# Expert weights in an MoE stage: successive rows to a partition, and transposes that read strided columns

## The chip, the cores and the metric

The kernel runs on one NeuronCore of one Trainium2 chip. The metric is the device time of one execution in microseconds (us); the time of a kernel is the median of several executions. All numbers are float32 at the kernel's boundary. Engines carry the names of the profile: PE is TensorE's matrix multiplication, PEld its weight loading, DVE VectorE, ACT ScalarE, POOL GpSimd, SP SyncE, which here only issues DMA transfers.

## The reference

The reference is a small network: a first block (two kinds of attention, a mixture of experts, a gate) and two hybrid layers. The change touches the mixture of experts alone:

```python
def expert_block(args):
    xb, e = args
    hdn = jax.nn.silu(xb @ w1[e]) * (xb @ w3[e])
    return hdn @ w2[e]
```

There are 1024 tokens of width 1024 and 32 experts; a router sends each token to two of them. `w1[e]` and `w3[e]` are 1024 x 512, `w2[e]` is 512 x 1024. `xb` holds up to 128 tokens of one expert. All weights of all experts are read once: 32 x 6 MB = 192 MB.

## The kernel before, in words

**Order of the work.** The kernel is written in the Tile framework. An automatic scheduler, which simulates a timeline, sets the order of instructions on each engine; the program gives the work in the order of `moe`'s loop, and the scheduler moves it where dependences and buffers allow.

**Rows of an expert.** For expert e, `gather` (L925) fetches its 128 token rows into `xg` with an indirect DMA on POOL's queue, two buffers in turn. `expert` then transposes them: eight 128x128 transposes on PE (L887), four to a PSUM bank, where block k takes the columns k*128 to k*128+127 of `xg`. The result is split into two float32r numbers that add up to it: ACT copies the high half to `exh` (L869), DVE subtracts for the low half `exl` (L871).

**Weights.** Each matrix comes as two tiles of 1 MB (128 partitions x 2048 numbers), named a and b here: for `w1` and `w3` the upper and lower 512 rows, for `w2` the left and right 512 columns. `fetch` has `load_raw` issue one DMA per tile on SP's queue (L122): row k*128+p of the tile goes to partition p, so each partition gets four runs of 2 KB. The raw tiles lie in seven buffers that take turns. `split` (PIECES = 4) cuts a tile into four pieces of 128x512; ACT copies the high half (L113), DVE subtracts the low one (L114). The halves go to two buffers `whi`/`wlo` in turn, or to the single buffer `mhi`/`mlo`; every third tile takes the latter. For an expert that gives: w1b to `m`, w3b to `w`, the next expert's w1a to `w` and w3a to `m`, w2a and w2b to `w`.

**Matmuls.** `mm` (L877 to L879) does one product of 128 rows in three matmuls of 512 columns: high x high, high rows x low weights, low rows x high weights. `w1` and `w3` take 8 x 3 each. ACT forms silu into `esg` (L904, two halves), DVE multiplies into `ehd` (L905, two halves); PE transposes `ehd` (four times, L910), which is split into `ehh` and `ehl` by the same lines L869 and L871. For `w2` there are two column halves c, each with a PSUM bank of its own: four k of three matmuls, then ACT copies the bank into `ey` (L919). POOL scatters the finished `ey` to DRAM with an indirect DMA (L920).

**The loop.** `moe` runs in its body for expert e: the transposes of e+1; w1b and w3b of e with `esg`, `ehd` and its transposes; w1a and w3a of e+1; in e = 4 to 11 a tile of other work (PLE, L643 ff); then w2a and w2b of e. `overflow` holds a loop for experts with over 128 rows; with these data it runs zero times. PSUM has five banks for matmuls and three for transposes.

Of the kernel before, what the change touches and what calls it, by code (L numbers as in the profile page):

```python
# [7 lines left out]
F32 = mybir.dt.float32  # L8
F32R = mybir.dt.float32r
I32 = mybir.dt.int32  # L10
AF = mybir.ActivationFunctionType
# [25 lines left out]
PLACE = (4, 7, 8)  # L37


MOE_RAW, MOE_HL, MOE_DMA, PIECES, PLE = 3, 1, 1, 4, 4  # L40

LATE = 7

# [1 line left out]
class Kernel:  # L45
# [70 lines left out]
    def load_raw(self, raw, src, kt, n, dma=2):  # L116

        raw = raw[:, :kt * n].rearrange("p (k n) -> p k n", n=n)
        s = src.rearrange("(k p) n -> p k n", p=128)
        st = kt // dma  # L120
        for j in range(dma):
            self.wdma = self.nc.sync.dma_start(raw[:, j * st:(j + 1) * st], s[:, j * st:(j + 1) * st])  # L122
        return raw

    def w_raw(self):
# [736 lines left out]
    def expert(self, wp, xg, w1, w3, w2, sidx, native, after=None):  # L862


        nc = self.nc
        dt = F32 if native else F32R

        def put(hi, lo, p):
            nc.scalar.activation(hi, p, AF.Copy)  # L869
            if not native:  # L870
                nc.vector.tensor_sub(lo, p, hi.bitcast(F32))  # L871

        def mm(ps, a, k, w, first, last):
            if native:
                nc.tensor.matmul(ps, a[0][:, k], w, start=first, stop=last)
                return
            nc.tensor.matmul(ps, a[0][:, k], w[0], start=first, stop=False)  # L877
            nc.tensor.matmul(ps, a[0][:, k], w[1], start=False, stop=False)
            nc.tensor.matmul(ps, a[1][:, k], w[0], start=False, stop=last)  # L879

        xh = wp.tile([128, 8, 128], dt, name="exh", bufs=1 if native else 2)
        xl = xh if native else wp.tile([128, 8, 128], F32R, name="exl", bufs=2)
        for hf in range(2):
            p = self.t_ps()
            for j in range(4):
                k = hf * 4 + j
                nc.tensor.transpose(p[:, j * 128:j * 128 + 128], xg[:, k * 128:k * 128 + 128], self.ident)  # L887
            put(xh[:, hf * 4:hf * 4 + 4].rearrange("p a t -> p (a t)"),
                xl[:, hf * 4:hf * 4 + 4].rearrange("p a t -> p (a t)"), p)
        yield  # L890
        qs = [self.mm_ps() for _ in range(2)]
        for c in range(2):
            for w, q in zip((w1, w3), qs):
                ww = w(c)
                for k in range(4):
                    mm(q, (xh, xl), c * 4 + k, ww[:, k] if native else (ww[0][:, k], ww[1][:, k]), c + k == 0, c + k == 4)
            if c == 0:
                yield
        hd = wp.tile([128, 512], F32, name="ehd", bufs=1)
        sg = wp.tile([128, 512], F32, name="esg", bufs=1)  # L900
        for c in range(2):
            cs = slice(c * 256, c * 256 + 256)
            with self.tc.issue_after(after.ins) if after else nullcontext():
                nc.scalar.activation(sg[:, cs], qs[0][:, cs], AF.Silu)  # L904
            nc.vector.tensor_mul(hd[:, cs], qs[1][:, cs], sg[:, cs])  # L905
        hh = wp.tile([128, 4, 128], dt, name="ehh", bufs=1)
        hl = hh if native else wp.tile([128, 4, 128], F32R, name="ehl", bufs=1)
        p = self.t_ps()
        for j in range(4):
            nc.tensor.transpose(p[:, j * 128:j * 128 + 128], hd[:, j * 128:j * 128 + 128], self.ident)  # L910
        put(hh.rearrange("p a t -> p (a t)"), hl.rearrange("p a t -> p (a t)"), p)
        yield
        y = wp.tile([128, D], F32, name="ey", bufs=1)
        for c in range(2):
            ww = w2(c)
            q = self.mm_ps()
            for k in range(4):
                mm(q, (hh, hl), k, ww[:, k] if native else (ww[0][:, k], ww[1][:, k]), k == 0, k == 3)
            nc.scalar.activation(y[:, c * 512:c * 512 + 512], q, AF.Copy)  # L919
        yield nc.gpsimd.indirect_dma_start(  # L920
            out=self.y_d[:, :], out_offset=bass.IndirectOffsetOnAxis(ap=sidx, axis=0), in_=y, in_offset=None,
            bounds_check=2 * SEQ - 1, oob_is_err=False)
# [6 lines left out]
    def overflow(self):  # L929

        tc, nc, I = self.tc, self.nc, self.I
        self.done = self.keep.tile([128, 1], F32, name="done")
        nc.vector.memset(self.done, 0.0)
        ov = self.dram.tile([128, 3, 16], I32, name="ov_d")
        nc.sync.dma_start(ov[:, 0], self.gidx[:, 32:48])
        nc.sync.dma_start(ov[:, 1], self.sidx[:, 32:48])
        nc.sync.dma_start(ov[:, 2], self.eid)
        n = nc.values_load(self.nov[0:1, 0:1], min_val=0, max_val=15)
        with self.banks(tp=3, mm=5), self.pool(name="ov", bufs=1) as wp:
            with tc.For_i(0, n, 1) as b:  # L940
                ix = wp.tile([128, 3], I32, name="ix")
                nc.sync.dma_start(ix, ov[:, :, bass.ds(b, 1)].rearrange("p c o -> p (c o)"))
                e = nc.values_load(ix[0:1, 2:3], min_val=0, max_val=31)
                xg = wp.tile([128, D], F32, name="oxg")
                nc.vector.memset(xg, 0.0)
                nc.vector.memset(self.done, 0.0)
                self.gather(xg, ix[:, 0:1])

                def w(name, rows):
                    def f(c):  # L950
                        t = wp.tile([128, 4, 512], F32, name="ow")
                        cs = slice(c * 512, c * 512 + 512)
                        src = I[name][0, bass.ds(e, 1)]
                        src = src[:, cs] if rows else src[:, :, cs]
                        nc.sync.dma_start(t, src.rearrange("o (k p) n -> p (o k) n", p=128))
                        return t
                    return f

                list(self.expert(wp, xg, w("w1", True), w("w3", True), w("w2", False), ix[:, 1:2], True))
        pre = nc.scalar.activation(self.done, self.done, AF.Copy)  # L960
        with tc.issue_after(pre.ins):
            return nc.scalar.preload_act_table_set("natural_log_exp_and_others")

    def moe(self, pgp):
        tc, nc, I = self.tc, self.nc, self.I
# [5 lines left out]
        raws, ws = {}, {}  # L971
        n = [0, 0]

        with self.pool(name="mraw", bufs=1) as rw, ExitStack() as xs:
# [6 lines left out]
            def fetch(key):  # L981
                e, nm, c = key
                j = n[0]
                n[0] += 1
                b = order[j] if j < NF else bufs[(j - NF) % len(bufs)]
                raw = b[0].tile([128, 2048], F32, name="mraw", tag=b[1]) if b else self.w_raw()
                cs = slice(c * 512, c * 512 + 512)
                raws[key] = self.load_raw(raw, I[nm][0, e][:, cs] if nm == "w2" else I[nm][0, e][cs], 4, 512, dma=MOE_DMA)

            def split(key, pieces=PIECES):  # L990
                n[1] += 1
                hl = (self.w_hl() if n[1] % (2 + MOE_HL) in (1, 2) else
                      [mw.tile([128, 2048], F32R, name="m" + t, bufs=MOE_HL) for t in ("hi", "lo")])
                ws[key] = self.split_w(raws.pop(key), hl, pieces)

            def weights(key):
                if key not in ws:
                    if key not in raws:
                        fetch(key)
                    split(key)  # L1000
                return ws.pop(key)


            for key in seq[:NF]:
                fetch(key)
            xp = self.pool(name="mxg", bufs=1)
            xgs = []
            with xp as xp, self.pool(name="mw", bufs=1) as mw:
                for j in range(2):
                    t = xp.tile([128, D], F32, name="xg%d" % j)  # L1010
# [3 lines left out]
                for j in range(2 + MOE_HL):  # L1014
                    split(seq[j], 4)
                    fetch(seq[NF + j])
                self.gates()
                last = self.last
                with self.banks(tp=3, mm=5), self.pool(name="mx", bufs=1) as wp, ExitStack() as ps:
                    sc = []  # L1020
                    def start(e):

                        if 2 <= e:
                            self.gather(xgs[e % 2], self.gidx[:, e:e + 1])
                        x = self.expert(wp, xgs[e % 2], *[lambda c, name=name: weights((e, name, c)) for name in ("w1", "w3", "w2")],
                                        self.sidx[:, e:e + 1], False, None if e else last)
                        next(x)
                        return x
# [3 lines left out]
                    for e in range(NE):  # L1032

                        if e + 1 < NE:
                            y = start(e + 1)
# [5 lines left out]
                        s = next(x)  # L1041
# [505 lines left out]
```

## Time and profile before

| | |
|---|---|
| median of 3 runs | 2946.88 us (2945.25 to 2947.84) |
| the profiled execution's own time | 2949.21 us |
| its span in the trace | 2947.4 us |
| mean granted clock of TensorE | 0.967 of full speed |
| PE busy over the span | 2710.2 us (92%) |
| DVE busy | 2127.2 us (72%) |
| ACT busy | 1760.7 us (60%) |
| read from HBM / written | 425.71 MB / 101.97 MB |
| experts: first and last `esg` start | 866.3 us, 1467.2 us |

The times are those of one profiled execution. Busy shares are averages over stages of very different kinds; the experts take about a fifth of the span. A busy PE is not PE at its peak, since matmuls are pipelined and overlap: a 512-column matmul is shown as 0.39 us long, while the next starts earlier. "Waits" name for each idle stretch of an engine the event that ended it.

### The profile page before, as it was taken

The page shows a single profiled execution, that of the slowest core. Times are in us where ns is not written, and L with a number is a line of the kernel's source. Part 1 is how long each engine was busy: PE and PEld are TensorE (multiplying, and loading weights), DVE is VectorE, ACT ScalarE, POOL GpSimd, SP SyncE. Part 2 cuts the span into 40 slices and gives each one's busy share as a digit, 9 for nine tenths or more (in the row PEclk, how much of TensorE's full clock was granted, in tenths as well). Part 3 has the DMA queues.
Part 4 walks back from the last instruction along what each step waited for, and adds up shares of the span by engine and source line. Part 5 has one row for each costly group of instructions (what it writes and reads, how often), then busy time and mean ns, then how long its engine had stood idle before and what let it go on. Part 6 is the DMA issues. An engine that isn't in the chain of part 4 may idle for free. (4 is left out here: it accounts for less than half of the span.)

```text
span 2947.4 us, 49384 instructions
## 1 busy us (share of the span) xinstructions
PE 2710.2 (92%) x17751; PEld 2447.2 (83%) x17751; DVE 2127.2 (72%) x4362; ACT 1760.7 (60%) x3827; POOL 718.0 (24%) x847
## 2 busy tenths in 40 slices
PE   7999889788979999999959799999989899999988
PEld 7998878678968777877749788999889788899888
DVE  6778589676389888999965458899355368898354
ACT  4444467554258878888846357788342367788242
POOL 0343131563001102111024101650123102650132
PEclk9999999889989999999979899999999899999999
DMA  7766432324279989999851333322562342331661
GB/s 237 248 204 204 130 79 69 64 50 141 109 272 328 314 313 355 368 363 367 308 211 70 115 120 96 98 87 75 199 217 73 116 128 88 98 95 65 223 190 72
DMA packets 390010, 512.92 MB, mean 174 GB/s; under 512 B 94948, under 2 KB 236284, under 8 KB 389252
## 3 DMA queue, kind: packets, MB, share of 16 engines
q1 hardware_dynamic: 375364, 480.37, 49.3%
q0 software_dynamic: 14400, 29.38, 3.0%
q8 instruction: 141, 2.31, 0.3%
q14 instruction: 105, 0.86, 0.1%
HBM read 425.71 MB, written 101.97 MB: 179 GB/s over the span
## 5 line engine op out<-in xcount | busy, mean ns | idle before, releaser
L150 PE MATMUL mm<-whi,acth 128*128 128x256 f32 x2816 | 812.0, 288 | 20.5 <-ACT acth L113 5.7
L152 PE MATMUL mm<-whi,actl 128*128 128x256 f32 x2816 | 807.4, 287 | 6.4 <-DVE rsx L100 3.8
L151 PE MATMUL mm<-wlo,acth 128*128 128x256 f32 x2816 | 804.8, 286 | 0.0
L150 PEld LDWEIGHTS mm<-whi,acth 128*128 128x128 f32 x2816 | 543.7, 193 | 31.7 <-ACT acth L113 7.9
L152 PEld LDWEIGHTS mm<-whi,actl 128*128 128x128 f32 x2816 | 542.6, 193 | 11.0 <-DVE rsx L100 4.3
L151 PEld LDWEIGHTS mm<-wlo,acth 128*128 128x128 f32 x2816 | 543.2, 193 | 3.0 <-issue 0.9
L114 DVE TENSOR_TENSOR wlo<-mraw,whi 128x512 fp32r<-128x512 f32 x508 | 316.1, 682 | 46.7 <-ACT whi L113 46.4
L113 ACT ACTIVATE whi<-mraw 128x512 fp32r<-128x512 f32 x508 | 276.1, 628 | 11.5 <-PE mm L879 9.3
L114 DVE TENSOR_TENSOR wlo<-wraw,whi 128x2048 fp32r<-128x2048 f32 (+1 forms) x64 | 145.5, 2278 | 138.9 <-ACT whi L113 129.1
L1198 PE MATMUL mm<-acth,whi 128*128 128x512 f32 x512 | 201.7, 394 | 0.0
L1200 PE MATMUL mm<-acth,wlo 128*128 128x512 f32 x512 | 201.1, 393 | 0.0
L1199 PE MATMUL mm<-actl,whi 128*128 128x512 f32 x512 | 200.5, 392 | 0.0
L113 ACT ACTIVATE whi<-wraw 128x2048 fp32r<-128x2048 f32 (+1 forms) x64 | 117.0, 1833 | 102.0 <-PE mm L152 67.6
L1240 POOL TENSOR_TENSOR cN<-rx,rcos 128x256 f32<-128x256 f32 x64 | 63.4, 990 | 444.2 <-ACT rx L1237 440.4
L114 DVE TENSOR_TENSOR mlo<-mraw,mhi 128x512 fp32r<-128x512 f32 x256 | 160.2, 680 | 2.9 <-ACT mhi L113 1.6
L1373 ACT ACTIVATE sw<-sw 128x128 f32<-128x128 f32 (+2 forms) x192 | 100.8, 528 | 70.5 <-DVE sw L1372 69.5
L113 ACT ACTIVATE mhi<-mraw 128x512 fp32r<-128x512 f32 x256 | 140.6, 631 | 2.9 <-PE mm L879 2.9
L920 POOL DMA_INDIRECT y_d<-ey,sidx x32 | 39.0, 1219 | 373.5 <-ACT ey L919 364.8
L1366 DVE SCALAR_TENSOR_TENSOR sw<-z,sw 128x128 f32<-128x128 f32 (+1 forms) x192 | 103.8, 547 | 30.3 <-ACT sw L1365 29.5
L1386 DVE TENSOR_TENSOR sal<-tp,sah 128x512 fp32r<-128x512 f32 (+1 forms) x192 | 101.8, 546 | 25.4 <-ACT sah L1385 24.8
L1363 ACT ACTIVATE sw<-z 128x128 f32<-128x128 f32 (+1 forms) x192 | 93.3, 491 | 38.2 <-DVE z L1360 38.0
L1200 PEld LDWEIGHTS mm<-acth,wlo 128*128 128x128 f32 x512 | 96.2, 188 | 19.6
(361 smaller groups left out, 6776.0 us busy)
## 6 DMA issues: line engine op xcount, KB each, us to landing
mraw<-in_w_dram SPq DMA_DIRECT2D x191, 1024.0 KB, 9.0
wraw<-in_w_in_dram SPq DMA_DIRECT2D x88, 512.0 KB, 4.8
mw<-in_w_ada_dram SPq DMA_DIRECT2D x32, 768.0 KB, 6.7
wraw<-in_w_out_dram SPq DMA_DIRECT2D x24, 512.0 KB, 5.3
q_d<-qo SPq DMA_DIRECT2D x32, 256.0 KB, 3.2
q<-q_d POOLq DMA_DIRECT2D x32, 256.0 KB, 2.9
h_d<-res SPq DMA_DIRECT2D x16, 512.0 KB, 2.7
sqk<-sq_d SPq DMA_DIRECT2D x32, 256.0 KB, 4.1
```

The lines of the kernel that those rows point to most:

```text
L113: nc.scalar.activation(hi, raw, AF.Copy)
L114: nc.vector.tensor_sub(lo, raw, hi.bitcast(F32))
L150: nc.tensor.matmul(ps[:, :n], ah[:, k, sl], wh[:, k, :n], start=k == 0, stop=False)
L151: nc.tensor.matmul(ps[:, :n], ah[:, k, sl], wl[:, k, :n], start=False, stop=False)
L152: nc.tensor.matmul(ps[:, :n], al[:, k, sl], wh[:, k, :n], start=False, stop=k == kt - 1)
L1198: nc.tensor.matmul(ps, wh[:, k, cs], hh[:, k], start=k == 0, stop=False)
L1199: nc.tensor.matmul(ps, wh[:, k, cs], hl[:, k], start=False, stop=False)
L1200: nc.tensor.matmul(ps, wl[:, k, cs], hh[:, k], start=False, stop=k == 7)
L1363: nc.scalar.activation(a, z, AF.Abs)
L1366: nc.vector.scalar_tensor_tensor(a, z, 0.0, a, op0=OP.max, op1=OP.add)
L1373: nc.scalar.activation(a, a, AF.Exp)
L1386: nc.vector.tensor_sub(al[ts], pv, ah[ts].bitcast(F32))
```

## The change

`load_rows` takes the place of `load_raw` for the experts' tiles: partition p gets k successive rows of the matrix (k = 4 for `w1` and `w3`, k = 2 for `w2`), which lie side by side in DRAM, so that a partition's share is one run of 8 KB. `w2` is cut by halves of its rows in place of its columns: tile a holds rows 0 to 255 with all 1024 columns. A matmul block k now pairs with every fourth (second) row of the matrix, so the transposes take every fourth column of `xg` and every second column of `ehd`. In the third product both PSUM banks are open over both tiles, and both copies to `ey` come after the loop. The cut into four pieces of 128x512 stays, as do all counts. `overflow`'s loader changes in the same way.

```diff
+    def load_rows(self, raw, src, k):
+        raw = raw.rearrange("p (k n) -> p k n", k=k)
+        self.wdma = self.nc.sync.dma_start(raw, src.rearrange("(p k) n -> p k n", k=k))
         return raw
...
             for j in range(4):
-                k = hf * 4 + j
-                nc.tensor.transpose(p[:, j * 128:j * 128 + 128], xg[:, k * 128:k * 128 + 128], self.ident)
+                nc.tensor.transpose(p[:, j * 128:j * 128 + 128], xg[:, hf * 512 + j:hf * 512 + 512:4], self.ident)
...
         for j in range(4):
-            nc.tensor.transpose(p[:, j * 128:j * 128 + 128], hd[:, j * 128:j * 128 + 128], self.ident)
+            nc.tensor.transpose(p[:, j * 128:j * 128 + 128], hd[:, j // 2 * 256 + j % 2:j // 2 * 256 + 256:2], self.ident)
...
+        qs = [self.mm_ps() for _ in range(2)]
         for c in range(2):
             ww = w2(c)
-            q = self.mm_ps()
-            for k in range(4):
-                mm(q, (hh, hl), k, ww[:, k] if native else (ww[0][:, k], ww[1][:, k]), k == 0, k == 3)
-            nc.scalar.activation(y[:, c * 512:c * 512 + 512], q, AF.Copy)
+            for k in range(2):
+                for n, q in enumerate(qs):
+                    ns = slice(n * 512, n * 512 + 512)
+                    mm(q, (hh, hl), c * 2 + k, ww[:, k, ns] if native else (ww[0][:, k, ns], ww[1][:, k, ns]),
+                       c + k == 0, c + k == 2)
+        for n, q in enumerate(qs):
+            nc.scalar.activation(y[:, n * 512:n * 512 + 512], q, AF.Copy)
...
-                cs = slice(c * 512, c * 512 + 512)
-                raws[key] = self.load_raw(raw, I[nm][0, e][:, cs] if nm == "w2" else I[nm][0, e][cs], 4, 512, dma=MOE_DMA)
+                k = 2 if nm == "w2" else 4
+                raws[key] = self.load_rows(raw, I[nm][0, e][c * 128 * k:c * 128 * k + 128 * k], k)
```

The scheduler also gives the engines another order, over the experts alone. Three places in the last dozen experts show it. Lines of the changed kernel lie 6 to 10 higher: L876 is L869 of before, L878 L871, L884 to L886 L877 to L879, L910 and L911 L904 and L905, L929 L919.

ScalarE, one expert of the last dozen, before: `mhi` first is w1b, the four `whi` are w3b, `esg` the expert's silu, the next four `whi` w1a of the following expert, `ey` the copies of the expert before; `mhi` at the end is w3a.

```order
L113 ACTIVATE mhi<-mraw 128x512 x4
L113 ACTIVATE whi<-mraw 128x512 x4
L904 ACTIVATE esg<-mm 128x256 x2
L113 ACTIVATE whi<-mraw 128x512 x4
L919 ACTIVATE ey<-mm 128x512 x2
L869 ACTIVATE exh<-tp 128x512 x2
L869 ACTIVATE ehh<-tp 128x512
L113 ACTIVATE mhi<-mraw 128x512 x4
```

The same stretch of ScalarE now:

```order
L113 ACTIVATE mhi<-mraw 128x512 x4
L929 ACTIVATE ey<-mm 128x512 x2
L910 ACTIVATE esg<-mm 128x256 x2
L113 ACTIVATE whi<-mraw 128x512 x8
L113 ACTIVATE mhi<-mraw 128x512 x4
L876 ACTIVATE exh<-tp 128x512 x2
L876 ACTIVATE ehh<-tp 128x512
```

What moved: `esg` stands ahead of all eight `whi` copies in place of between the two fours, `ey` ahead of `esg`, where it is the one of two experts before, and w3a's `mhi` stands ahead of `exh`.

TensorE, the end of the third product of one expert and the beginning of w1b (`mhi`, `mlo`) of the next, before:

```order
L878 MATMUL mm<-wlo,ehh 128x512
L879 MATMUL mm<-whi,ehl 128x512
L877 MATMUL mm<-mhi,exh 128x512
L878 MATMUL mm<-mlo,exh 128x512
L879 MATMUL mm<-mhi,exl 128x512
```

The same products on TensorE now, the end of w1b, where the first bank of the third product has been finished ahead of it (its last two matmuls stand just behind w1b's first):

```order
L885 MATMUL mm<-mlo,exh 128x512
L886 MATMUL mm<-mhi,exl 128x512
L884 MATMUL mm<-whi,ehh 128x512
L885 MATMUL mm<-wlo,ehh 128x512
L886 MATMUL mm<-whi,ehl 128x512
```

What moved: before, all 24 matmuls of the third product stand ahead of w1b; now the twelve of the first bank do, w1b's twelve follow, and the twelve of the second bank come behind them, ahead of w3b.

VectorE, from `ehd` to the third product's low pieces, before:

```order
L905 TENSOR_TENSOR ehd<-mm,esg 128x256 x2
L114 TENSOR_TENSOR wlo<-mraw,whi 128x512 x3
L871 TENSOR_TENSOR exl<-tp,exh 128x512 x2
L871 TENSOR_TENSOR ehl<-tp,ehh 128x512
L114 TENSOR_TENSOR mlo<-mraw,mhi 128x512 x4
L114 TENSOR_TENSOR wlo<-mraw,whi 128x512 x8
```

The same stretch of VectorE now:

```order
L911 TENSOR_TENSOR ehd<-mm,esg 128x256 x2
L114 TENSOR_TENSOR wlo<-mraw,whi 128x512
L114 TENSOR_TENSOR mlo<-mraw,mhi 128x512 x4
L878 TENSOR_TENSOR exl<-tp,exh 128x512 x2
L878 TENSOR_TENSOR ehl<-tp,ehh 128x512
L114 TENSOR_TENSOR wlo<-mraw,whi 128x512 x8
```

What moved: w3a's `mlo` stands ahead of `exl` and `ehl` in place of behind them, and `ehd` behind seven of the eight low pieces of w3b and w1a in place of five.

## Rows read from the trace of the kernel before

**Rows 1.** Windows: busy us (x instructions) of PE, PEld, DVE, ACT, POOL; PEclk; DMA share; GB/s
```profile
865.00:938.00 73.00, 72.63 (x350) 59.87 (x350) 69.98 (x132) 63.11 (x122) 7.85 (x8) 1.00 0.86 308
938.00:1115.00 177.00, 174.30 (x764) 133.15 (x762) 147.47 (x250) 139.26 (x291) 18.18 (x16) 1.00 0.91 324
1115.00:1222.00 107.00, 104.54 (x492) 85.58 (x491) 99.30 (x170) 92.86 (x182) 22.45 (x12) 1.00 1.00 360
1222.00:1460.00 238.00, 228.58 (x1065) 186.42 (x1064) 216.91 (x369) 198.69 (x394) 23.21 (x23) 1.00 1.00 364
```
**Rows 2.** Waits, 938 to 1115 us: engine, line, releaser: us in total, times, longest
```profile
PEld mm L877 <- ACT whi L113: 4.4, 4, 1.2
...
PE mm L877 <- ACT whi L113: 2.7, 4, 0.7
```
**Rows 3.** Waits, 1240 to 1456 us
```profile
PEld mm L878 <- DVE mlo L114: 13.1, 12, 1.1
...
DVE ehd L905 <- PE mm L879: 9.8, 12, 0.8
DVE wlo L114 <- ACT whi L113: 9.8, 12, 0.8
```
**Rows 4.** Timeline, one late expert: start us, us, engine, line, operation, count, [idle before]
```profile
1280.49 0.66 ACT L904 ACTIVATE esg<-mm 128x256 f32<-128x256 f32 x2 [2.48 <-PE mm L879]
...
1281.03 2.19 ACT L113 ACTIVATE whi<-mraw 128x512 fp32r<-128x512 f32 x4
...
1281.70 0.69 DVE L114 TENSOR_TENSOR wlo<-mraw,whi 128x512 fp32r<-128x512 f32 x1 [0.81 <-ACT whi L113]
...
1283.12 1.08 ACT L919 ACTIVATE ey<-mm 128x512 f32<-128x512 f32 x2
1283.21 0.76 DVE L905 TENSOR_TENSOR ehd<-mm,esg 128x256 f32<-128x256 f32 x2 [0.82 <-PE mm L879]
...
1284.14 1.04 PE L887 MATMUL tp<-ident,xg 128*128 128x128 f32 x8
...
1285.72 1.28 DVE L871 TENSOR_TENSOR exl<-tp,exh 128x512 fp32r<-128x512 f32 x2
...
1289.93 4.89 DVE L114 TENSOR_TENSOR wlo<-mraw,whi 128x512 fp32r<-128x512 f32 x8
...
1290.41 0.39 PE L878 MATMUL mm<-mlo,exh 128*128 128x512 f32 x1
...
1292.45 0.39 PE L878 MATMUL mm<-wlo,ehh 128*128 128x512 f32 x1
...
1294.74 2.48 DVE L114 TENSOR_TENSOR mlo<-mraw,mhi 128x512 fp32r<-128x512 f32 x4
1297.15 2.48 DVE L114 TENSOR_TENSOR wlo<-mraw,whi 128x512 fp32r<-128x512 f32 x4
1299.22 0.38 ACT L904 ACTIVATE esg<-mm 128x256 f32<-128x256 f32 x1 [2.47 <-PE mm L879]
```
**Rows 5.** Loads: issue and landing of `mraw`; SP's issues; window of a later stretch (columns of rows 1)
```profile
mraw<-in_w_dram SPq DMA_DIRECT2D x191, 1024.0 KB, 9.0
...
DMA to landing us min/median/max: 5.2/9.0/14.1
...
1254.95 45.08 SPq L122 DMA_DIRECT2D mraw<-in_w_dram  x16
...
2094.00:2100.00 6.00, 6.00 (x28) 4.95 (x28) 2.29 (x1) 2.40 (x2) 0.00 (x0) 1.00 1.00 403
```
**Rows 6.** Groups by form, VectorE's sums: L712 strided, L733 contiguous: busy us, mean ns
```profile
L712 DVE TENSOR_REDUCE ee<-pr 128x32 f32<-128x128 f32 x1 | 0.4, 369 | 0.0
L712 DVE TENSOR_REDUCE ee<-pr 128x8 f32<-128x32 f32 x1 | 0.2, 196 | 0.0
...
L733 DVE TENSOR_REDUCE rank<-big 128x8 f32<-128x256 f32 x1 | 0.4, 420 | 0.0
L733 DVE TENSOR_REDUCE rank<-big 128x2 f32<-128x64 f32 x1 | 0.2, 219 | 0.0
```

More of the change, by code (lines that the diff above doesn't have):

```diff
@@ L37 @@
 PLACE = (4, 7, 8)
-MOE_RAW, MOE_HL, MOE_DMA, PIECES, PLE = 3, 1, 1, 4, 4
+MOE_RAW, MOE_HL, PIECES, PLE = 3, 1, 4, 4
 LATE = 7
@@ L122, in load_raw @@
             self.wdma = self.nc.sync.dma_start(raw[:, j * st:(j + 1) * st], s[:, j * st:(j + 1) * st])
+        return raw
+    def load_rows(self, raw, src, k):
+        raw = raw.rearrange("p (k n) -> p k n", k=k)
+        self.wdma = self.nc.sync.dma_start(raw, src.rearrange("(p k) n -> p k n", k=k))
         return raw
@@ L947, in overflow, with w @@
                 self.gather(xg, ix[:, 0:1])
-                def w(name, rows):
+                def w(name, k):
                     def f(c):
-                        t = wp.tile([128, 4, 512], F32, name="ow")
-                        cs = slice(c * 512, c * 512 + 512)
-                        src = I[name][0, bass.ds(e, 1)]
-                        src = src[:, cs] if rows else src[:, :, cs]
-                        nc.sync.dma_start(t, src.rearrange("o (k p) n -> p (o k) n", p=128))
+                        t = wp.tile([128, k, 2048 // k], F32, name="ow%d" % k)
+                        src = I[name][0, bass.ds(e, 1)][:, c * 128 * k:c * 128 * k + 128 * k]
+                        nc.sync.dma_start(t, src.rearrange("o (p k) n -> p (o k) n", k=k))
                         return t
                     return f
-                list(self.expert(wp, xg, w("w1", True), w("w3", True), w("w2", False), ix[:, 1:2], True))
+                list(self.expert(wp, xg, w("w1", 4), w("w3", 4), w("w2", 2), ix[:, 1:2], True))
         pre = nc.scalar.activation(self.done, self.done, AF.Copy)
@@ L986, in fetch @@
                 raw = b[0].tile([128, 2048], F32, name="mraw", tag=b[1]) if b else self.w_raw()
-                cs = slice(c * 512, c * 512 + 512)
-                raws[key] = self.load_raw(raw, I[nm][0, e][:, cs] if nm == "w2" else I[nm][0, e][cs], 4, 512, dma=MOE_DMA)
+                k = 2 if nm == "w2" else 4
+                raws[key] = self.load_rows(raw, I[nm][0, e][c * 128 * k:c * 128 * k + 128 * k], k)
             def split(key, pieces=PIECES):
@@ L993, in split @@
                       [mw.tile([128, 2048], F32R, name="m" + t, bufs=MOE_HL) for t in ("hi", "lo")])
-                ws[key] = self.split_w(raws.pop(key), hl, pieces)
+                raw = raws.pop(key)
+                k = raw.shape[1]
+                ws[key] = [t.rearrange("p (k n) -> p k n", k=k) for t in hl]
+                raw, (hi, lo) = raw.rearrange("p k n -> p (k n)"), hl
+                s = 2048 // pieces
+                for j in range(0, 2048, s):
+                    self.split(*(t[:, j:j + s] for t in (raw, hi, lo)))
             def weights(key):
```

## The prediction, made before the changed kernel was timed

> **What bounds the kernel now.** I read the windows view over the experts first, since the change touches nothing else. [rows 1] give four stretches: experts 0 to 3, experts 4 to 11 (a tile of other work rides along with each), 12 to 17, and from 1222 us on the last dozen. [...] TensorE is busy 99.5, 98.5 and 97.7% of the first three and 96.0% of the last; the DMA engines are at 1.00 in the last two, which makes the weights' loads the first suspect.
>
> The waits view sorts this out. In experts 4 to 11 TensorE and its weight loads wait 7.1 of 177 us [rows 2]: there TensorE's own work is the bound. In the last stretch TensorE waits about once per expert for VectorE's low halves (`mlo`, 13.1 us in 12 waits), and VectorE waits twice, for ScalarE's copy and for TensorE [rows 3]. No row of either answer that is longer than 0.2 us names a transfer of weights.
>
> The timeline of one late expert shows its pace [rows 4]. From one `esg` (1280.49) to the next (1299.22) are **18.73 us**. VectorE does 24 low pieces at 0.60 us start to start (8 in 4.89 us), three more of the same length (`exl` twice, `ehl`; two in 1.28) and two `ehd` at 0.33: 14.4 + 1.8 + 0.7 = 16.9 us. It idles 0.81 us before a `wlo`, because that piece's copy on ScalarE stands behind the two `esg`, and 0.82 us before `ehd`: 18.5, with 0.2 of small gaps the whole cycle. So VectorE, with two short waits, sets the pace late. TensorE needs 72 matmuls at 0.227 us (nine steps from 1290.41 to 1292.45) and 12 transposes at 0.11 (eight in 1.04): 16.3 + 1.3 = 17.6 us; that is its floor.
>
> Are the loads the bound all the same? 16 of them are issued in 45.08 us, one each 3.0 us, when VectorE frees a buffer [rows 5]. Seven buffers take turns over six tiles an expert, so a turn lasts 7/6 x 18.73 = 21.9 us; some four of these the splitting takes (2.19 us for four pieces on ScalarE, 2.48 on VectorE behind it, [rows 4]), so about 17 remain between issue and need. Loads land after 9.0 us in the middle and 14.1 at most [rows 5]. A full share here means that about three loads are always under way, not that anyone waits for them.
>
> **The loads, part by part.** The same 192 MB in the same number of instructions, a packet of 8 KB for four of 2 KB. I have no row for 1 MB in 8 KB runs on this queue; the nearest is a later stretch, in the hybrid layers, where the loads have runs of 4 KB and the share is also 1.00, at 403 GB/s [rows 5], against 360 to 364 over the experts with a full share [rows 1]. Faster transfers would land earlier in a slack of 3 us or more: **0 us**. If the cover went, each us by which a load came late would cost up to 1 us on an expert.
>
> **The new order on the three computing engines.** No engine gains or loses an instruction; but the scheduler has set them anew from expert 0 on, because the third matrix now needs both row halves before either result is whole. In the last experts (the printed pieces) three things differ. (a) `ey` comes a cycle late: it copies expert e-2 where it copied e-1. (b) `esg` now stands ahead of all eight `whi` copies, those of w3b and of the next w1a, where it stood between the two. (c) TensorE runs the two halves of the third matrix apart, with w1b between them, since the second bank waits for the late `ey`.
>
> What (b) and (c) cost I follow by hand. VectorE starts on w1b's `mlo` at 0 and is free at 2.41 (1297.15 less 1294.74 in its timeline; four pieces at 0.60). The first piece is ready at 0.68, so TensorE starts its second w1b matmul at 0.73 (0.05 us for the signal: ScalarE's first `whi` copy, 1281.03 and 0.63 long, ends 0.04 ahead of VectorE's 1281.70, [rows 4]). Ten steps of 0.227 and 0.39 for the last: w1b ends at 3.39, the two `esg` run from 3.44 to 4.10 (0.66 for two). The next `whi` copy needs the buffer of w2a, read by the first six matmuls of the second sweep: started at 3.23, the sixth at 4.36, over by 4.75. Copy from 4.80 to 5.43, VectorE resumes at 5.48. It has idled **3.07 us in place of 0.81 + 0.82**; the wait before `ehd` is gone, as seven pieces (4.2 us) now lie ahead of it. Per expert 3.07 - 1.63 = +1.4 us. The settled form holds for seven experts (23 to 29); 19 to 22 have mixed forms with `ey` already late, and I price them the same: 11 x 1.44 = **+16 us**. Bounds: +5 if the mixed forms and half of the settled ones cost nothing, 12 x 2 = +24 if the late `ey` also holds up a bank. Behind the waiting `whi` copies stand only ScalarE's own next copies; SP's loads wait for VectorE's buffers, up to 1.4 us longer, inside the slack above; POOL's scatters of y follow `ey` a cycle later, and each gather behind them fetches rows for a transpose two experts on: 0 for both queues.
>
> The third printed piece moves w3a's `mlo` ahead of `exl` and `ehl`. That takes away the wait of 13.1 us in 12 [rows 3], but TensorE doesn't pace this stretch any more: 0 us. It also covers the transposes here with 2.4 us of VectorE's work. In experts 0 to 17 TensorE stays the bound and its count is the same: 0, at best the 7.1 us of [rows 2], at worst +8.
>
> **The copies at the end.** Both `ey` (1.08 for two) follow the last matmul where one did: **+0.5 us** [rows 4].
>
> **The strided weight loads.** A transpose has the rows as TensorE's weights; xg is now read with a step of 16 bytes, `ehd` with one of 8. No row before shows a strided weight load. The lower bound is the contiguous price, 0.11 a transpose [rows 4]: +0. The nearest rows are VectorE's: sums over strided columns (32 bytes, L712) take (369 - 196)/96 = 1.80 ns an element, over contiguous ones (L733) (420 - 219)/192 = 1.05, x1.7 [rows 6]. I take x1.7 for the 16-byte step: 0.08 more on each of eight, 0.64 us an expert where TensorE is the bound, 17 experts (intervals between 0 and 17): **+10 us**. In the late stretch it is covered by the `mlo` ahead of `exl` (2.4 us against 0.64); uncovered it would be 12 x 0.64 = 8 more. Doubled, 17 x 8 x 0.11 = +15. The 8-byte step I take as free; at x1.7 four more transposes would add 17 x 4 x 0.08 = +5.
>
> [...]
>
> **Sum.** 2949.2 us (the profiled execution's own time; its span is 2947.4, and it is 2.3 above the median of 2946.9) + 0 + 16 + 0.5 + 10 = 2975.7; on the scale of the median **2973 us**, 0.9% slower.
>
> **Rivals.**
> 1. Strided weight loads are free, the order costs its 16: 2946.9 + 16.5 = 2963. For: nothing in the trace shows TensorE slowed by a step; VectorE's strided sums are over 4 elements each and the contiguous ones over 32, which alone may explain x1.7. Against: [rows 6] as they stand.
> 2. Each strided load of xg takes double its 0.11 us: 2946.9 + 16.5 + 15 = 2978; with `ehd` at x1.7 too, 2983. For: VectorE's x1.7 is an average that holds fixed costs of an element as well. Against: TensorE's weights come 128 columns in 0.11 us, and no row shows what holds that up. [...]
> 3. Faster, by the order: in the last stretch the `mlo` ahead of `exl` takes away the only wait of TensorE there, and VectorE's wait is no longer than before, so that TensorE's floor of 17.6 sets the pace: 12.7 x (18.73 - 17.6) = -14, 2933. It is decided at VectorE's `wlo` behind `esg`: if the buffer of w2a is free and `esg` done within 1 us of VectorE's last `mlo`, this holds. For: the wait is there in 12 of 12 [rows 3], and the printed piece does move the `mlo` ahead. Against: my chain puts that point at 3.07.
> 4. Faster, by the loads: the share of 1.00 is the bound after all; 4 KB rows would give 18.73 x (1 - 364/403) = 1.8 us an expert, stopped by TensorE's floor at the same 2933. Against: nobody waits for a load [rows 2, 3].
> 5. The loads turn late: copies behind `esg` free the raw buffers later in bursts, and landing rises past the 17 us. Each us beyond, on 12 experts, is 12; two make 2997.
> 6. The edit alters nothing that binds: the late copies are made up by TensorE, whose floor leaves 1.1 us an expert, and strided loads cost nothing: 2947, within 0.2%.
>
> **How the numbers follow.** A measurement of this kernel can tell about 0.2%, 6 us, from no change. Chances: the forecast 0.37; strided free 0.30; doubled 0.12; loads late 0.06; no change 0.07; faster by the order 0.05, by the loads 0.03. So slower 0.85, same 0.07, faster 0.08. The range leaves out cases 3 to 6, about 0.2, and takes in the bounds inside the others: from 2946.9 + 5 + 5 = 2957 (a small price of the order and half of the strided one) up to rival 2 with the order's upper part, 2988.
>
> **What would show it.** In the changed kernel's profile: expert to expert about 20.2 us late in the stretch, with VectorE's first `wlo` after w1b's `mlo` waiting some 3 us for ScalarE's `whi`, and `esg` waiting for TensorE ahead of it; no wait for `mraw` on any computing engine; the transposes of xg at 0.19 us start to start instead of 0.11, `ehd`'s at 0.11; experts 0 to 17 longer by 0.6 us each; packets of 8 KB at over 400 GB/s with a DMA share below 1.00. It is wrong if late experts stay at 18.7 or less, if the transposes keep 0.11 us (then 2963), or if the loads' landing time shows up as a wait.

## The result, and the profile after

The changed kernel takes 2967.21 us (median of 4 runs, 2965.83 to 2969.7) against 2946.07 us for the kernel before; the ratio is 1.0072 with an interval of 1.0056 to 1.0087. That is 21 us slower, between 16 and 26. The forecast was 2973 in a range of 2957 to 2988.

The page of the changed kernel, busy times, DMA packets and the loads' issues (last number: median us to landing):

```profile
PE 2724.9 (92%) x17751; PEld 2452.5 (83%) x17751; DVE 2124.7 (72%) x4362; ACT 1761.9 (59%) x3827; POOL 753.1 (25%) x847
...
DMA packets 316282, 512.92 MB, mean 173 GB/s; under 512 B 94948, under 2 KB 236284, under 8 KB 290948
...
mraw<-in_w_dram SPq DMA_DIRECT2D x191, 1024.0 KB, 7.4
```

No engine has more instructions. The packets fell from 390010 to 316282, that is by 73728 = 192 x (512 - 128), so all loads have 8 KB packets; they land after 7.4 us where they took 9.0 [rows 5]. The time was lost all the same.

Where it was lost, from the starts of the transposes of `ehd` in both profiled executions:

| experts | before, us | after, us | difference |
|---|---|---|---|
| 0 to 4 | 73.1 | 73.6 | +0.5 |
| 4 to 12 | 174.5 | 179.4 | +4.9 |
| 12 to 18 | 107.1 | 104.6 | -2.5 |
| 18 to 23 | 93.7 | 100.4 | +6.7 |
| 23 to 30 | 131.3 | 141.1 | +9.8 |
| 30 to 31 | 17.3 | 16.4 | -0.9 |

That is +18.4 of the 20.3 by which the two spans differ; the rest changes sign from stage to stage elsewhere. The first and last start of these transposes, first in the kernel before and then in the changed one, give the length of the whole experts' stretch, 597.6 and 616.1 us:

```profile
L910 PE MATMUL tp<-ident,ehd x128: 270/272/330, 873.0 to 1470.6; 128*128 128x128 f32 x128
```

```profile
L916 PE MATMUL tp<-ident,ehd x128: 270/282/386, 871.5 to 1487.6; 128*128 128x128 f32 x128
```

The last stretch first, as windows (columns as in [rows 1]), of the changed kernel:

```profile
1250.00:1440.00 190.00, 179.88 (x788) 136.16 (x786) 162.69 (x278) 149.10 (x294) 34.59 (x18) 1.00 0.92 342
```

VectorE is busy 162.7 of 190 us, 85.6%, where it was 91% in the last stretch of before [rows 1]; the DMA share is 0.92 at 342 GB/s where it was 1.00 at 364. With longer runs and a slower pace the DMA engines are no longer full. What VectorE and TensorE wait for there, by the waits view:

```profile
DVE wlo L114 <- ACT whi L113: 25.5, 9, 4.2
ACT esg L910 <- PE mm L886: 22.0, 8, 4.4
PEld mm L885 <- DVE wlo L114: 21.6, 39, 0.7
ACT whi L113 <- PE mm L886: 12.0, 8, 5.3
PEld mm L885 <- DVE mlo L114: 6.8, 8, 0.9
```

Nine waits of VectorE for ScalarE's `whi`, 2.8 us each, have taken the place of one of 0.8 us per expert [rows 3]; the wait before `ehd` is gone from the top of the list. The timeline of one expert of this stretch, VectorE and ScalarE, and of TensorE one matmul and the transposes:

```profile
1341.69 0.66 ACT L910 ACTIVATE esg<-mm 128x256 f32<-128x256 f32 x2 [2.51 <-PE mm L886]
...
1342.63 0.39 PE L886 MATMUL mm<-whi,ehl 128*128 128x512 f32 x1
...
1343.05 4.28 ACT L113 ACTIVATE whi<-mraw 128x512 fp32r<-128x512 f32 x8 [0.70 <-PE mm L886]
1343.72 4.30 DVE L114 TENSOR_TENSOR wlo<-mraw,whi 128x512 fp32r<-128x512 f32 x7 [3.10 <-ACT whi L113]
1347.94 0.75 DVE L911 TENSOR_TENSOR ehd<-mm,esg 128x256 f32<-128x256 f32 x2
...
1349.85 1.13 PE L893 MATMUL tp<-ident,xg 128*128 128x128 f32 x8
```

The first four lines are the chain of the prediction: VectorE idles 3.10 us before `wlo`. ScalarE is free 0.70 us earlier than it copies: it ends `esg` at 1342.35 and still waits for TensorE until 1343.05, that is for the second sweep over w2a to let go of its buffer (the matmul shown is the sixth of that sweep and ends at 1343.02). So of the two things on that path the buffer is the later. Then eight transposes of strided columns take 1.13 us in place of 1.04 [rows 4].

### The profile page after: what moved, and what is told of

Same layout as the page of the kernel before. It is cut to its first block, busy times and chain, and to the rows that moved or that the text cites. A ratio compares the mean times of both kernels' runs of the same rounds, so it can differ in the third digit from the quotient of the medians.

```text
span 2967.7 us, 49379 instructions
## 1 busy us (share of the span) xinstructions
PE 2724.9 (92%) x17751; PEld 2452.5 (83%) x17751; DVE 2124.7 (72%) x4362; ACT 1761.9 (59%) x3827; POOL 753.1 (25%) x847
## 2 busy tenths in 40 slices
DMA packets 316282, 512.92 MB, mean 173 GB/s; under 512 B 94948, under 2 KB 236284, under 8 KB 290948
## 4 chain that ended last, share of the span: by engine, by line
PE 24%; DVE 13%; ACT 5%; DMA 4%; issue 3%; POOL 1%; SPq 0%; DVEq 0%; ACTq 0%; POOLq 0%
PE mm L1212 3%; PE mm L1213 3%; PE mm L1214 3%; PE mm L156 3%; PE mm L158 3%; PE mm L157 3%; DVE sw L1381 3%; DVE sw L1380 1%; DVE sal L1400 1%; DMA sqk<-sk_d 1%; DVE sw L1386 1%; DVE wlo L114 1%; DVE actl L114 1%; ACT sw L1377 1%; PE tp L1396 1%
## 5 line engine op out<-in xcount | busy, mean ns | idle before, releaser
L114 DVE TENSOR_TENSOR mlo<-mraw,mhi 128x512 fp32r<-128x512 f32 x256 | 160.3, 684 | 16.5 <-ACT mhi L113 16.2
L1387 ACT ACTIVATE sw<-sw 128x128 f32<-128x128 f32 (+2 forms) x192 | 100.9, 528 | 74.2 <-DVE sw L1386 73.1
L935 POOL DMA_INDIRECT xg<-xf_d,gidx x32 | 47.1, 1472 | 364.5 <-PE tp L893 176.4
L930 POOL DMA_INDIRECT y_d<-ey,sidx x32 | 65.7, 2054 | 239.1 <-ACT ey L929 233.5
L1380 DVE SCALAR_TENSOR_TENSOR sw<-z,sw 128x128 f32<-128x128 f32 (+1 forms) x192 | 103.8, 548 | 30.8 <-ACT sw L1379 30.1
```

The source lines that it names most:

```text
L114: nc.vector.tensor_sub(lo, raw, hi.bitcast(F32))
L1380: nc.vector.scalar_tensor_tensor(a, z, 0.0, a, op0=OP.max, op1=OP.add)
L1387: nc.scalar.activation(a, a, AF.Exp)
```

## The experiments

**The change in four parts.** The loads, the strided reads and the new w2 can be had apart. Four kernels on one chip; before took 2947.38 us there.

The first keeps `w2` as before:

```diff
-                k = 2 if nm == "w2" else 4
-                raws[key] = self.load_rows(raw, I[nm][0, e][c * 128 * k:c * 128 * k + 128 * k], k)
+                if nm == "w2":
+                    raws[key] = self.load_raw(raw, I[nm][0, e][:, c * 512:c * 512 + 512], 4, 512, dma=1)
+                else:
+                    raws[key] = self.load_rows(raw, I[nm][0, e][c * 512:c * 512 + 512], 4)
```

with the third product and `ehd`'s transposes of before.

> w1 and w3 as in the change (8 KB runs, strided xg transposes), w2 as before (column halves, 2 KB runs, contiguous transposes of ehd, one bank at a time). The order of every engine but SP's loads is that of the kernel before. Theory 'order' (what costs is the new order that w2 by row halves brings): within 3 us of before, 8 transposes x 17 experts x 0.012 us = +1.6. Theory 'strides': +10 us or more. Theory 'loads': faster than before, up to -13 us.

It took 2947.28 us, ratio 1.0001 (0.9988 to 1.0013). In the time of the kernel, two thirds of the 8 KB loads and all strided transposes of `xg` come to nothing.

The second is the reverse: `load_rows` for `w2` alone, `load_raw` and contiguous columns for `w1`, `w3` and `xg`.

> w2 as in the change (row halves, 8 KB runs, two banks open, strided transposes of ehd), w1 and w3 as before. The order on ACT, PE, DVE and POOL is that of the changed kernel, instruction by instruction. Theory 'order': all of the change's cost is here, +18 to +21 us, with late experts at 20.1 us. Theory 'strides' (of xg): half of the cost is missing, +10. Theory 'loads late': less than the change.

It took 2971.6 us, ratio 1.0076 (1.0061 to 1.0091): the whole cost of the change. Its transposes of `xg` are 0.109 us apart. The waits of its last stretch (1250 to 1440 us) are those of the changed kernel:

```profile
DVE wlo L114 <- ACT whi L113: 25.5, 9, 4.2
PEld mm L885 <- DVE wlo L114: 23.4, 44, 0.8
ACT esg L910 <- PE mm L886: 22.3, 8, 4.4
```

The third and fourth move the strided reads alone, out of the changed kernel and into the one before:

```diff
-                nc.tensor.transpose(p[:, j * 128:j * 128 + 128], xg[:, hf * 512 + j:hf * 512 + 512:4], self.ident)
+                nc.tensor.transpose(p[:, j * 128:j * 128 + 128], xg[:, (hf * 4 + j) * 128:(hf * 4 + j) * 128 + 128], self.ident)
```

and the same for `ehd`.

> The changed kernel with both sets of transposes reading contiguous columns; so the transposed rows are paired with other rows of the weights than in the reference. The order is that of the changed kernel on all five engines. Theory 'order': 1 to 3 us faster than the changed kernel (transposes back at 0.109 us start to start), still +17 to +20 on before. Theory 'strides': +11 or less on before.

It took 2967.9 us, ratio 1.0067 (1.0052 to 1.0081), against 1.0072 (1.0056 to 1.0087) for the changed kernel: no difference that can be told.

> The kernel before with both sets of transposes reading strided columns as in the change, and nothing else; rows and weights are paired otherwise than in the reference. The order is that of before. Theory 'order': +0 to +3 us, transposes at 0.12 us start to start. Theory 'strides': +10 us or more.

It took 2947.46 us, ratio 1.0000 (0.9989 to 1.0011). That bounds the price of all strided reads at +3.3 us. The weight loads by line show the step plainly (min/median/max ns of one): the kernel before, then this one, `xg`; then `ehd` before and in the changed kernel.

```profile
L887 PEld LDWEIGHTS tp<-ident,xg x256: 138/141/231, 852.3 to 1434.9; 128*128 128x128 f32 x128
...
L910 PEld LDWEIGHTS tp<-ident,ehd x128: 137/141/148, 872.8 to 1470.5; 128*128 128x128 f32 x128
```

```profile
L886 PEld LDWEIGHTS tp<-ident,xg x256: 195/211/230, 853.9 to 1437.8; 128*128 128x128 f32 x128
```

```profile
L916 PEld LDWEIGHTS tp<-ident,ehd x128: 194/198/217, 871.3 to 1487.5; 128*128 128x128 f32 x128
```

A strided load is recorded half as long again, 211 ns for 141. But loads overlap with other work: eight of 211 ns one behind the other would be 1.69 us, and the eight transposes of the changed kernel take 1.13 in all. What counts is the distance of two starts: 0.109 us contiguous, 0.121 strided (medians of 189 pairs each). On eight transposes that is 0.1 us an expert.

The experts' stretch alone shows this price, as the granted clock is 1.00 in every window of it, from 865 to 1460 us in the kernel before [rows 1] and from 865 to 1480 in the changed one. The third kernel (contiguous columns in the changed kernel), then the fourth (strided columns in the kernel before):

```profile
L916 PE MATMUL tp<-ident,ehd x128: 270/272/330, 875.6 to 1490.0; 128*128 128x128 f32 x128
```

```profile
L909 PE MATMUL tp<-ident,ehd x128: 270/282/385, 874.4 to 1473.6; 128*128 128x128 f32 x128
```

That is 614.4 us in place of 616.1 and 599.2 in place of 597.6: 1.7 and 1.6 us for all strided reads.

**The loads alone.** The kernel before, with 8 KB runs:

```diff
-                cs = slice(c * 512, c * 512 + 512)
-                raws[key] = self.load_raw(raw, I[nm][0, e][:, cs] if nm == "w2" else I[nm][0, e][cs], 4, 512, dma=MOE_DMA)
+                k = 2 if nm == "w2" else 4
+                raws[key] = raw.rearrange("p (k n) -> p k n", n=512)
+                self.wdma = nc.sync.dma_start(raw, I[nm][0, e][c * 128 * k:c * 128 * k + 128 * k].rearrange("(p k) n -> p (k n)", k=k))
```

> The kernel before with all three matrices loaded in 8 KB runs and nothing else; rows and weights are paired otherwise than in the reference. The order of ACT, PE, DVE and POOL is that of before. Theory 'order': landing falls to about 7.4 us as in the changed kernel, time within 3 us of before, since no engine waits for a load. Theory 'loads bound' (DMA share of 1.00): -13 us.

It took 2949.93 us, ratio 1.0006 (0.9995 to 1.0018); before took 2947.85 beside it. Its windows over the last two stretches, against the third and fourth of [rows 1]:

```profile
1115.00:1222.00 107.00, 105.27 (x495) 86.52 (x496) 99.32 (x170) 90.73 (x179) 22.07 (x12) 1.00 0.96 363
1222.00:1460.00 238.00, 228.62 (x1065) 186.40 (x1064) 216.89 (x369) 200.72 (x398) 23.14 (x23) 1.00 0.94 360
```

In the same 238 us VectorE does 216.89 us of work where it did 216.91, while the DMA share falls from 1.00 to 0.94. Nobody used the room. The landing times can't be compared in this trace, which doesn't hold them.

**What in the new order costs.** Five runs: three leave the loads and the strides of the change in place, two try the cause on the kernel before.

Six PSUM banks for matmuls and two for transposes:

```diff
-                with self.banks(tp=3, mm=5), self.pool(name="mx", bufs=1) as wp, ExitStack() as ps:
+                with self.banks(tp=2, mm=6), self.pool(name="mx", bufs=1) as wp, ExitStack() as ps:
```

> The changed kernel with six PSUM banks for matmuls and two for transposes in place of five and three. Theory 'bank' (the second bank of w2 waits for ey of the expert before, since five banks must serve two of w1 and w3 for two experts and two of w2; so w1b is put between the two halves of w2, which holds w2a's buffer): with six the wait of 3.1 us before wlo goes, late experts fall from 20.1 to 18.7 or less, the kernel is at 2947 or below, down to 2935 where TensorE's floor of 17.6 us is met. Theory 'esg' (the order of esg ahead of w3b's copies costs it, whatever the banks): stays at +15 to +20. Theory 'transposes need three banks': slower than the changed kernel.

It took 2937.82 us, ratio 0.9962 (0.9949 to 0.9975), faster than before. Late experts take 18.2 us. On TensorE both halves of w2 stand ahead of w1b again, and on ScalarE `esg` between the fours of `whi`. Waits of the stretch from 1250 to 1440 us:

```profile
DVE ehd L911 <- PE mm L886: 8.6, 9, 2.1
DVE wlo L114 <- ACT whi L113: 4.8, 9, 2.4
PEld mm L885 <- DVE mlo L114: 3.0, 8, 0.4
```

VectorE's wait of 25.5 us is down to 4.8.

The control, the same line in the kernel before:

> The kernel before with six PSUM banks for matmuls and two for transposes. A control: before opens one bank of w2 at a time, so theory 'bank' gives it less than the changed kernel, 0 to -6 us; if it gains as much as the changed kernel does (over 15 us), the banks have nothing to do with the change.

It took 2931.22 us, ratio 0.9934 (0.9920 to 0.9949), the lowest time of all. It gained 17 us, much more than I expected, and by the letter of my condition ("over 15 us") that would leave the banks without a part in the change. But the condition was put on the whole time, and the experts' stretch says otherwise. This kernel, then the changed one with six banks:

```profile
L910 PE MATMUL tp<-ident,ehd x128: 270/272/328, 872.9 to 1465.6; 128*128 128x128 f32 x128
```

```profile
L916 PE MATMUL tp<-ident,ehd x128: 270/283/385, 875.5 to 1466.7; 128*128 128x128 f32 x128
```

With six banks the kernel before takes 592.7 us over the experts in place of 597.6, that is 4.9 less and inside the 0 to 6 that theory 'bank' gave it; the changed kernel takes 591.2 in place of 616.1, that is 24.9 less. The other 12 us of the control's gain lie behind the last expert: from 1465.6 to the end of its span of 2930.6 are 1465.0 us, where the kernel before takes 1476.8. All four kernels with six banks take 1463.1 to 1468.4 us there and all others 1469.8 to 1480.9, and in these four alone GpSimd's order behind the experts is another one. Which instructions there bring the 12 us isn't shown. The waits over the last experts (1250 to 1440 us), in this kernel and then in the kernel before:

```profile
DVE ehd L905 <- PE mm L879: 8.2, 10, 0.8
...
DVE wlo L114 <- ACT whi L113: 5.1, 10, 0.6
PEld mm L878 <- DVE mlo L114: 5.0, 10, 0.5
```

```profile
PEld mm L878 <- DVE mlo L114: 12.6, 11, 1.1
...
DVE wlo L114 <- ACT whi L113: 8.2, 10, 0.8
```

TensorE's wait for `mlo` falls from 12.6 to 5.0 us and VectorE's for `whi` from 8.2 to 5.1: late experts take 18.5 us in place of 18.7. Experts 4 to 12 take 171.4 us in place of 174.5, 12 to 18 105.1 in place of 107.1; 0 to 4 lose 3.5. So six banks are better for either kernel, but in the experts they give the changed one five times as much, of which 18.5 us undo what the change had added.

The order of `esg`:

```diff
     def split(self, raw, hi, lo):
...
-        nc.scalar.activation(hi, raw, AF.Copy)
+        self.sp = nc.scalar.activation(hi, raw, AF.Copy)
...
+        sp = None if native else self.sp
         for c in range(2):
             cs = slice(c * 256, c * 256 + 256)
-            with self.tc.issue_after(after.ins) if after else nullcontext():
+            with self.tc.issue_after((after or sp).ins) if after or sp else nullcontext():
```

> The changed kernel with esg issued on ScalarE behind the copies of w3b's split, as before had it; the scheduler may move other instructions too. Theory 'bank': the next copy waits for the buffer of w2a until 4.80 us, 0.70 us after esg's end, so where TensorE's order stays (w1b between the halves of w2) nothing is gained; gain only if TensorE's order changes with it. Theory 'esg': late experts back to 18.7 us, the kernel within 5 us of before.

It took 2947.27 us, ratio 0.9998 (0.9989 to 1.0007). The cost is gone from the late experts, which take 18.7 us again, and from the time of the kernel. But TensorE's order changed with it: the scheduler now puts both halves of w2 ahead of w1b, with the same five banks. So it is no proof for `esg` alone. Nor is the experts' stretch as a whole that of before: it takes 604.1 us in place of 597.6, since experts 4 to 18 lose 10.6 us and 18 to 23 gain 4.6. What makes up for the 6.5 us in the rest of the kernel isn't shown.

The order of w1b on TensorE, the opposite handle:

```diff
                 for k in range(4):
-                    mm(q, (xh, xl), c * 4 + k, ww[:, k] if native else (ww[0][:, k], ww[1][:, k]), c + k == 0, c + k == 4)
+                    with self.tc.issue_after(self.w2l.ins) if c == 1 and k == 0 and w is w1 and self.w2l and not native else nullcontext():
+                      mm(q, (xh, xl), c * 4 + k, ww[:, k] if native else (ww[0][:, k], ww[1][:, k]), c + k == 0, c + k == 4)
```

where `w2l` is the last matmul of w2 of the expert before.

> The changed kernel, five banks, with the first matmul of w1b issued on TensorE behind the last of w2 of the expert before. Theory 'settled pattern' (w1b between the halves of w2 is what the scheduler has fallen into, it keeps w2a's buffer and brings esg forward; the five banks themselves don't cost it): late experts at 18.7 us, total within 4 us of before. Theory 'bank' in its strict form (five banks are too few for two open ones): w2's second half waits for a bank, +10 us or more remain.

It took 2953.93 us, ratio 1.0017 (1.0005 to 1.0028): 5 us, a little over the 4 that theory 'settled pattern' allowed. ScalarE's order fell back into the old form by itself. VectorE's timeline of a late expert is that of [rows 4] again, two waits of 0.8 us, ahead of them `mlo` of w1b and `wlo` of w3b without a gap:

```profile
1302.46 2.48 DVE L114 TENSOR_TENSOR mlo<-mraw,mhi 128x512 fp32r<-128x512 f32 x4
1304.87 2.48 DVE L114 TENSOR_TENSOR wlo<-mraw,whi 128x512 fp32r<-128x512 f32 x4
1308.15 0.69 DVE L114 TENSOR_TENSOR wlo<-mraw,whi 128x512 fp32r<-128x512 f32 x1 [0.80 <-ACT whi L113]
1309.66 0.76 DVE L912 TENSOR_TENSOR ehd<-mm,esg 128x256 f32<-128x256 f32 x2 [0.82 <-PE mm L886]
```

Late experts take 18.7 us; the experts' stretch is 4.0 us longer than before, and experts 0 to 4 alone take 77.7 us in place of 73.1. Five banks serve two open ones of w2 without a loss late in the stretch, so the strict form of the bank theory falls.

Its other side, the kernel before with four banks (`mm=4`):

> The kernel before with four PSUM banks for matmuls in place of five (three for transposes, one unused). Before needs one open bank of w2 beside two each for two experts. Theory 'bank' strict: one bank too few gives the same kind of cost as in the change, +15 us or so. Theory 'settled pattern': the count alone doesn't do it, within 5 us of before.

It took 2947.45 us, ratio 1.0002 (0.9989 to 1.0015). One bank fewer costs the old w2 nothing: the count alone is not the cause either.

**Versions that beat both.** The parts of the change that cost nothing, with six banks:

> w1 and w3 as in the change, w2 as before, six banks for matmuls and two for transposes. Both theories: as the kernel before with six banks, 2931 within 4 us, since neither the longer runs nor the strided transposes are worth anything here; if loads bind once the order is better, up to 5 us below that.

It took 2932.91 us, ratio 0.9948 (0.9929 to 0.9966).

> The changed kernel with six banks and esg behind w3b's copies. Late experts 18.2 us as with six banks alone; experts 12 to 18 a few us better by the scheduler's order. 2933 to 2938; if it were below 2931 it would beat every version so far.

It took 2935.69 us, ratio 0.9954 (0.9937 to 0.9971). All four kernels with six banks lie within 7 us; the intervals of the other three overlap or touch that of the fastest, the old loads with six banks. Experts 12 to 18 take 103.8 us in the last version and 103.9 with six banks alone, so the gain that I expected there from `esg` didn't come. Over the experts alone the last version is the fastest of all, 589.9 us; so the changed loads and the new w2 are no hindrance there once the order is a good one.

## Why the prediction was right, and where it wasn't

**What bounds the kernel: right.** The loads had slack. Longer runs land 1.6 us sooner in the changed kernel and lower the DMA share (0.94 at the pace of before), and the time doesn't move (1.0006 alone). Rival 4 falls, and rival 5 too: no computing engine waits for `mraw` in the waits of the changed kernel. The rate of over 400 GB/s that I named as a sign was not seen (342 in the late window, 360 with the loads alone): with DMA shares of 0.92 and 0.94 the kernel asked for no more at that pace. A share of 1.00 said that transfers were always under way, as the prediction put it.

**The price of the new order, +16: right in place and mechanism, and in size for the settled experts.** It was priced for experts 19 to 29; the table gives +6.7 + 9.8 = +16.5 from 18 to 30. By hand VectorE was to idle 3.07 us; it idles 3.10. Settled experts were to take 1.4 us more and 20.2 in all; they take +1.4 and 20.1, and with that rival 6 falls. For the mixed forms, experts 19 to 22, the nearness is luck: they were priced at 1.4 each without following them, and take 0.3, 1.3, 2.5 and 3.3 more. That the order carries the cost is shown: two kernels with the changed order on the four computing queues cost +0.76% and +0.67%, whatever their transposes read, and three with the old order cost 0.00 to +0.06%, whatever they load and read; and two kernels with all of the changed edit and five banks, but an order in which `esg` and w1b stand as before, have late experts of 18.7 us. That w2 alone brings it is shown by the second kernel.

**Which of the two moves costs, and why the scheduler makes them.** (b) `esg` first and (c) w1b between the halves came and went together in the late experts of every run, from whichever end they were held. The timeline has the buffer of w2a as the later of the two by 0.70 us, which speaks for (c) as the one that ends the wait; a kernel with one and not the other wasn't tried. The prediction named the late `ey` and its bank as the reason why w1b comes between. That stays open: with five banks both orders exist, and the scheduler's own reasons weren't measured.

**Experts 0 to 17, 0 with bounds of -7 and +8: right within its bounds.** Together they moved by +2.9: +0.5, +4.9 and -2.5. The prediction gave no mechanism for the parts; they belong to the order too, since the second and third kernels, with contiguous `xg` columns, have them as well (experts alternate between 23.8 and 20.9 us in 4 to 11 there, 24.0 and 20.9 in the changed kernel). All of the +4.9 lies in experts 4 to 7; the kernel before takes 22.4 from 8 to 11, which is what 24.0 and 20.9 come to. The lower bound of -7 was too wide from the start: it added the waits of PEld and of PE for the same copies [rows 2], while PE idles 2.7 us there [rows 1].

**The strided weight loads, +10: wrong.** This is the term that was mis-sized. The step was "I take x1.7 for the 16-byte step: 0.08 more on each of eight". Measured are 0.012 us each, 17 x 8 x 0.012 = 1.6 us; the experts' stretch shows 1.6 and 1.7, and the time of the kernel nothing that can be told (1.0000, up to +3.3 us). Two errors lie in it. VectorE's sums over 4 and over 32 elements are not a price for TensorE's reads, as rival 1 said. And even the right ratio of durations, 211/141 = x1.5, would have been the wrong one, for the loads overlap; the spacing is x1.11. Rival 1, with 2963, was the better forecast: 16.5 for the order and nothing for the steps, and what it lacks is within the measurement. Rival 2, with its doubled loads, falls.

The prediction took the 8-byte step as free, and rival 2's +15 took the 16-byte step as a doubled load; no run shows either. A load is recorded as 198 ns with a step of 8 bytes and as 211 with 16, against 141, and start to start the two come to 0.118 and 0.121 us, against 0.109. That VectorE's x1.7 holds fixed costs of an element, as rival 2 argued, was my estimate, and no run shows it.

**`ey` at the end, +0.5:** too small to be told from the rest.

**The rival on the other side** (faster by the `mlo` ahead of `exl`) held in one half: TensorE's wait of 12.6 us for the low pieces of `mhi` in the stretch from 1250 to 1440 us is 6.8, but 21.6 us for those of `whi` came in its place, and VectorE's wait of 3.10 us, where it was to be decided, exceeds the 1 us that was named.

**The sum.** 16 + 0.5 + 10 = 26.5 was forecast; 21.1 came, with an interval of 16 to 26. The order's 16.5 and the +2.9 of experts 0 to 17 make most of it. That 2973 lies only 6 us above the measured time is in part luck, since of its +10 for strides less than 2 came, and other stretches, priced at 0, filled in. The upper bound, rival 2 with the order's 24, comes to 2946.9 + 24 + 0.5 + 15 = 2986 on the scale of the median and not to 2988, which alters nothing here.

## What to carry to other kernels

Ahead of a change to transfers, ask how long a load lies ready before its first reader: with 17 us between issue and need, neither a DMA share of 1.00 nor a shorter landing says that anything will move. When an automatic scheduler sets the order, a change to one product's accumulation can cost more by the order that it brings than anything in the edit itself; so print both orders, follow one cycle by hand from the engine that sets the pace, and hold the one instruction that slid. When a lever moves the whole time, see in which stretch the time moved: of the control's 17 us, 12 lay where the lever wasn't meant to act. For operations that overlap, take the distance of two starts as the price (here 0.012 us more), not the duration of a record (0.070 more), and not a ratio from another engine.

## What the runs showed of the hardware that was not expected

A weight load of 128 strided float32 columns is recorded as 211 ns (step of 16 bytes) or 198 ns (8 bytes) where a contiguous one takes 141, and yet the transposes of `xg` start 0.121 us apart in place of 0.109 (of `ehd` 0.118). Of the 70 ns by which the record of an `xg` load is longer, 12 show in the distance of two starts.

Moving one PSUM bank from transposes to matmuls is worth 0.66% (0.51 to 0.80) of the time of the kernel before, and taking one away from the matmuls costs nothing (1.0002). Of the 0.66%, 4.9 us lie in the experts and about 12 behind them, where the scheduler's order has changed too; so this is no price of a bank, but of the orders that the scheduler finds with it.
